# Compressed-block attention: the empty rows zeroed through the gate instead of a mask product, and all evictions of the second v half on ScalarE

## The chip, the core and the metric

The kernel runs on one core of a Trainium2 chip. The core has five engines with a queue each: TensorE (PE in the profile; PEld is its weight load), VectorE (DVE), ScalarE (ACT), GpSimd (POOL) and SyncE (SP), which issues DMAs. The metric is the device time of one execution in microseconds; of several executions the median counts.

## The reference, cut to what matters

Two layers of a decoder trunk on 512 tokens of width 1024 in float32: a convolution module with a SwiGLU feed-forward layer (FFN), then native sparse attention with another FFN. The change lies in the attention, in its branch over compressed blocks:

```
def masked_softmax(s, mask):
    s = jnp.where(mask, s.astype(jnp.float32), NEG_INF)
    return jax.nn.softmax(s, axis=-1) * mask.astype(jnp.float32)
...
    gates = jax.nn.sigmoid(proj[..., qd + kvd:].astype(jnp.float32)).reshape(bsz, seq, 3, H)
...
        s_c = jnp.einsum('bgrqd,bgnd->bgrqn', qc, k_cmp) * scale
        p_c = masked_softmax(s_c, cmp_end[None, :] <= t[:, None])
        o_c = jnp.einsum('bgrqn,bgnd->bgrqd', p_c, v_cmp)
...
        return g[0] * o_c + g[1] * o_s + g[2] * o_w
```

There are 31 compressed blocks of 32 tokens at a stride of 16. The first 31 tokens have no finished block: all their scores are masked, and p_c is zero there. With 512 tokens the selected and the window branch (o_s, o_w) each see every earlier token. There are 16 heads in 4 groups of keys and values.

## The kernel before, in words

Activations lie transposed in SBUF, as 8 tiles of 128 features by 512 tokens. Weights come by DMA in units of 128x1024, and each unit is split into a high part (ScalarE, tile wh) and a low part (VectorE, tile wl, function w_lo), so that three fast matmuls make one of nearly full precision.

The attention (function nsa) has these stages. First the projections to k and q, one tile of 128 features after the other. Then the projections to v and to the gates, in two halves: v_half(0) makes the first v and the gates, v_half(1) the second v. Each half runs over three weight units and four tiles of tokens (t = 0 to 3), and ends with v_evac, which brings the four results from PSUM to SBUF with a scale per token; EVAC_V says for each half which t VectorE takes, the others go to ScalarE. Third comes a loop over n = 1 to 17 that works 16 units: for each of 8 head pairs j (two heads of two groups) the selected and the window branch. In step n PE makes the scores of unit n (function score, tile S; par is the head of the pair, t the tile of query tokens, in the order 3, 2, 1, 0), transposes the probabilities of unit n-1 (function flip, PSUM tile T, SBUF tile t) and multiplies those of unit n-2 with v (function values, tile O). Behind each score, VectorE adds the mask and takes the extremum in one instruction (Pm<-S,mask, with mx), ScalarE takes the Exp with the row sum (Pm, sm), VectorE the reciprocal of sm, and GpSimd scales Pm by it and by the gate (function weigh, called some way behind through weigh_late). The score tiles rotate through three PSUM buffers in the loop: two of pool apS, and one of apS2, which is opened in the place of a bank that held the second v half.

The compressed branch is worked for two tiles j at a time, by q_pair(p), p = 0 to 3: scores makes 128 x 4 x 2 x 64 scores (tile sc; psc in PSUM), soft_a takes the maximum (cm) and the difference on VectorE and lets ScalarE take the Exp, soft_b multiplies with the mask of ones and zeros (C_CMUL, on GpSimd), soft_c takes the row sum (cl), the maximum of it with 0.5, the reciprocal and the product with the gate on VectorE, and scales sc by it on GpSimd; trans transposes the result (pct, pch, pcl) for its product with the compressed v. stacks makes the stacked q operands (tile St, part of it on GpSimd for p > 0).

The order of the work is written out by hand: every instruction between the second q tile and the end of the loop is kept in the order of the program on its engine. Pieces named by short words are hung into it. V_BESIDE gives for v_half(0) and v_half(1), for each weight unit and each t, what is issued ahead of that t's matmuls: for pair 0, "sa sb" (soft_a, soft_b) ahead of t = 1 in the second unit of v_half(0), with "r13" (a rotation of q, tiles qraw), "c1" (a chain of small VectorE instructions, rsy) and "w" (w_lo of the next unit) behind them; "gb" (the last part of the gates' sigmoid) and "sc cu" (soft_c, then what was put off) in v_half(1). FILL gives what run_fill issues, twice in each step of the loop: the first time ahead of the two flips that VectorE copies, the second time at the end of the scores, ahead of the flips that ScalarE copies. "P1.2" is the third part of pair 1: for pairs 1 to 3, part 2 is the move of q and soft_a, part 3 is stacks and soft_b, part 4 is soft_c, part 5 is trans. Parts 2 and 4 fall into the second slot of a step, part 3 into the first slot of the next one. What is wrapped in behind(...) is put off to the next run_fill, whose first act it is (catch_up): so soft_a's Exp is issued on ScalarE at the start of the slot in which part 3 runs, behind the first transposes' copy.

Of the kernel before, what the change touches and what calls it, by code (L numbers as in the profile page):

```python
# [10 lines left out]
F32 = mybir.dt.float32  # L11
# [4 lines left out]
ALU = mybir.AluOpType  # L16
AX = mybir.AxisListType
PSUM = bass.MemoryType.PSUM

P = 128  # L20
# [23 lines left out]
C_CMUL = C_CADD + 256  # L44
# [44 lines left out]
V_BESIDE = (  # L89
    (("w r12", "st0", "p2m", "sABCD a1"), ("w sa sb", "t1", "r13 c1", ""), ("w", "", "", "")),  # L90
    (("ga", "w", "s0", "s1 b1"), ("", "s2 s3 w", "gb s4 l", "s5 st1"), ("s6 l", "s7 l", "sc cu", "")))
EVAC_V = ((1, 3), (1, 3))
V_BANK = (2, 3, 0, 1)
STK_P = (0,)

# [53 lines left out]
def trunk(ctx: ExitStack, tc: tile.TileContext, A, out):  # L149
    order = [False]  # L150
    nc = Engines(tc, order)
# [9 lines left out]
    def nm(s):  # L161
        cnt[0] += 1
        return f"{s}_{cnt[0]}"
# [118 lines left out]
    cc = cst.tile([P, NCST], F32, name="cc")  # L282
# [820 lines left out]
    def nsa(acc, cosT, sinT, gnext):  # L1103
        cx = ExitStack()

        def pool(cxx, name, bufs, **kw):
            return cxx.enter_context(tc.tile_pool(name=name, bufs=bufs, **kw))
# [80 lines left out]
        qk = pool(qx, "qk", 1, side="right", reuse_waits="tile")  # L1188
# [21 lines left out]
        box = {}  # L1210
# [37 lines left out]
        def behind(f):  # L1248

            if box.get("steps"):  # L1250
                later.append(f)
            else:
                f()
# [132 lines left out]
        def pe(ins):  # L1386
            return ins if order[0] else tc.keep_in_program_order(ins)

        def q_pair(p):

            a = p // 2
            sc = qk.tile([P, 4, 2, 64], F32, tag="sc", name=nm("sc"), bufs=1)

            def move(jj):
                q = oT[2 * p + jj]
                box["q2", jj] = []
                for par in range(2):
                    hs = slice(par * 64, par * 64 + 64)
                    q2 = qk.tile([P, T], F32, tag="q2", name=nm("q2"), bufs=Q2B)
                    for half in range(2):  # L1400
                        nc.sync.dma_start(q2[half * 64:half * 64 + 64], q[hs])
                    box["q2", jj].append(q2)

            def stacks(jj):
                j = 2 * p + jj
                S2 = qk.tile([P, 1088], F32R, tag="S", name=nm("St"), bufs=3)
                for par in range(2):
                    ls = slice(64 - par * 64, 128 - par * 64)
                    q2 = box["q2", jj][par]
                    S = S2[:, par * T:par * T + T]  # L1410
                    if p > 0 and par in STK_P:
                        nc.gpsimd.tensor_copy(S, q2)
                        nc.gpsimd.tensor_tensor(S[ls], q2[ls], S[ls], ALU.subtract)
                    else:
                        nc.scalar.activation(S, q2, AF.Copy)
                        behind(lambda S=S, q2=q2, ls=ls: nc.vector.tensor_tensor(S[ls], q2[ls], S[ls], ALU.subtract))
                    qst[j, par] = S

            def scores(jj):
                q = oT[2 * p + jj]  # L1420
                ps = p2.tile([P, 4, 64], F32, tag="p2", name=nm("psc"))
                for t in range(4):
                    pe(nc.tensor.matmul(ps[:, t, :], q[:, t * P:(t + 1) * P], kcb[a], start=True, stop=True))
                nc.vector.scalar_tensor_tensor(
                    sc[:, :, jj, :], ps, -1.0,
                    cc[:, C_CADD:C_CADD + 256].rearrange("p (t n) -> p t n", t=4), ALU.mult, ALU.add)

            def soft_a():
                s3 = sc.rearrange("p t j (h n) -> p (t j h) n", h=2)
                m = qk.tile([P, 16 + APART], F32, tag="cm", name=nm("cm"), bufs=1)[:, :16]  # L1430
                nc.vector.tensor_reduce(m, s3, AX.X, ALU.max)
                nc.vector.tensor_tensor(s3, s3, m.unsqueeze(2).to_broadcast([P, 16, 32]), ALU.subtract)
                sf = sc.rearrange("p t j n -> p (t j n)")
                behind(lambda: nc.scalar.activation(sf, sf, AF.Exp))

            def soft_b():
                s5 = sc.rearrange("p t j (h n) -> p t (j h) n", h=2)
                nc.gpsimd.tensor_tensor(
                    s5, s5, cc[:, C_CMUL:C_CMUL + 128].rearrange("p (t n) -> p t n", t=4)
                    .unsqueeze(2).to_broadcast([P, 4, 4, 32]), ALU.mult)  # L1440

            def soft_c():
                s3 = sc.rearrange("p t j (h n) -> p (t j h) n", h=2)
                l = qk.tile([P, 16], F32, tag="cl", name=nm("cl"), bufs=1)
                nc.vector.tensor_reduce(l, s3, AX.X, ALU.add)
                nc.vector.tensor_scalar(l, l, 0.5, None, ALU.max)
                nc.vector.reciprocal(l, l)
                r0 = 2 * (p % 2)
                gv = gates[:, :, 8 * a:8 * a + 8].rearrange("p t (h r) -> p t r h", h=2)[:, :, r0:r0 + 2, :]
                lv = l.rearrange("p (t j h) -> p t j h", t=4, j=2)  # L1450
                nc.vector.tensor_tensor(lv, lv, gv, ALU.mult)
                nc.gpsimd.tensor_tensor(
                    s3, s3, l.unsqueeze(2).to_broadcast([P, 16, 32]), ALU.mult)

            def trans():
                pt = p2.tile([P, T], F32, tag="p2", name=nm("pct"))
                for t in range(4):
                    pe(nc.tensor.transpose(pt[:, t * P:(t + 1) * P], sc[:, t].rearrange("p j n -> p (j n)"), ident))
                ph = q3[1].tile([P, T], F32R, tag="pch", name=nm("pch"))
                pl = q3[1].tile([P, T], F32R, tag="pcl", name=nm("pcl"))  # L1460
                nc.scalar.activation(ph, pt, AF.Copy)
                behind(lambda: nc.vector.tensor_tensor(pl, pt, ph, ALU.subtract))
                pcT[p] = (ph, pl)

            if p == 0:
                return move, scores, stacks, soft_a, soft_b, soft_c, trans
            return [lambda: (move(0), scores(0)), lambda: (stacks(0), scores(1)), lambda: (move(1), soft_a()),
                    lambda: (stacks(1), soft_b()), soft_c, trans]

        extra, bcs = {}, {}  # L1470
# [72 lines left out]
        for e in range(2, 14):  # L1543
# [7 lines left out]
            n = state["next"]  # L1551
# [18 lines left out]
        gates = ap_.tile([P, 4, 48], F32, name="gates")  # L1570
# [15 lines left out]
        def v_evac(hf, pst):  # L1586
            br = 1 + hf
            z = vf[br] = ap_.tile([P, 4, 256], F32, tag="w1v", name=f"v{br}", bufs=2)
            for t in range(4):
                ps = pst[t]  # L1590
                r1 = rt[:, t:t + 1]
                if t in EVAC_V[hf]:
                    nc.vector.tensor_scalar(z[:, t], ps[:, :256], r1, None, ALU.mult)
# [19 lines left out]
        def sigm_b():  # L1613
            g2 = gates.rearrange("p a b -> p (a b)")
            nc.vector.tensor_scalar(g2, g2, 1.0, None, ALU.add)
            nc.vector.reciprocal(g2, g2)

        extra["ga"] = sigm_a
        extra["gb"] = sigm_b
# [222 lines left out]
    acc = ffn(acc, V_NM1, 0, lambda: rope.extend(rope_tables()))  # L1842
    cosT, sinT = rope
    acc = nsa(acc, cosT, sinT, V_NF1)
    ffn(acc, None, 1)
    hx[0].close()
# [162 lines left out]
```

## Time and profile before

| what | value |
|---|---|
| median of 3 runs | 1217.6 us (1212.36, 1217.6, 1219.96) |
| the profiled execution: time, span | 1220.19 us, 1218.4 us |
| granted TensorE clock, mean | 1.000 |
| PE busy, 650 to 690 us | 37.16 of 40 us |
| PE busy, 690 to 720 us | 28.21 of 30 us |
| PE busy, 760 to 800 us | 38.52 of 40 us |
| PE busy, 870 us to the end (output projection, second FFN) | 343.43 of 348.40 us |

The span runs from the first to the last instruction of the profiled execution. In a row of a timeline the columns are: start in us from the span's start, duration in us, engine, line, operation, output <- inputs by the names of the tiles, shape, count, and in brackets the idle time of the engine ahead of it with what ended it. Nearly all rows have line 136, that of the helper which records each instruction, so the tiles tell which is which. A row of the chain gives the start, the time that the piece adds to the chain, the engine and the tile. In a row of the waits stand the waiting instruction, what it waited for, the total in us, the number of times and the longest. The durations of matmuls are modelled, and one may start before the one ahead of it shows its end.

### The profile page before, as it was taken

The numbers are of one execution on the slowest core, as the hardware profiler recorded it, in microseconds if no ns is written. First come the engines' busy times: TensorE is split into PE (matmuls) and PEld (weight loads), VectorE is DVE, ScalarE is ACT, GpSimd is POOL, SyncE is SP. The second block draws the span as 40 slices with busy tenths as digits, with TensorE's granted clock in tenths as the row PEclk, the third lists the DMA queues.
The fourth block names the chain that finished last, engine by engine and source line by source line (L and its number), as shares of the span: only waits on it lengthen the run. The fifth ranks groups of instructions, "written<-read, shape, count | busy, mean of one in ns | idle before, by whom it ended". The sixth has DMA issues, their size and how long they took to land.

```text
span 1218.4 us, 20771 instructions
## 1 busy us (share of the span) xinstructions
PE 1193.8 (98%) x8015; PEld 1021.8 (84%) x8015; DVE 813.0 (67%) x1453; ACT 560.9 (46%) x1048; POOL 373.2 (31%) x403
## 2 busy tenths in 40 slices
PE   9999899999999999999999999999999999999998
PEld 6888678799999988888778767778879999998887
DVE  6879687878788665334677778764597766656221
ACT  6222454454455543233434687773354555544111
POOL 1039021144444301101232577752213444410000
PEclk9999999999999999999999999999999999999999
DMA  9636336346677323334354211112634877722331
GB/s 365 245 107 142 78 102 192 104 128 184 173 182 182 95 89 108 97 116 109 112 127 121 62 40 30 28 36 70 190 104 117 220 186 185 187 81 96 115 113 45
DMA packets 81539, 154.25 MB, mean 127 GB/s; under 512 B 36128, under 2 KB 37024, under 8 KB 80672
## 3 DMA queue, kind: packets, MB, share of 16 engines
q1 hardware_dynamic: 66096, 109.04, 28.7%
q0 software_dynamic: 15344, 43.88, 15.3%
q8 instruction: 63, 1.03, 0.4%
q14 instruction: 36, 0.29, 0.1%
HBM read 139.37 MB, written 5.28 MB: 119 GB/s over the span
## 4 chain that ended last, share of the span: by engine, by line
PE 76%; issue 8%; POOL 6%; DVE 6%; ACT 3%; DMA 1%; SPq 0%; POOLq 0%; DVEq 0%; ACTq 0%
PE st L136 35%; PE pp L136 28%; POOL S L136 6%; PE cpe L136 2%; PE O L136 2%; PE S L136 2%; PE pv L136 2%; PE T L136 2%; ACT Pm L136 1%; DVE Pm L136 1%; DVE c L136 1%; DVE t L136 1%; POOL Pm L136 1%; DVE St L136 0%; PE psc L136 0%
## 5 line engine op out<-in xcount | busy, mean ns | idle before, releaser
L136 ACT ACTIVATE wh<-wr 128x1024 fp32r<-128x1024 f32 (+3 forms) x158 | 160.4, 1015 | 294.5 <-PE st L136 140.2
L136 DVE TENSOR_TENSOR wl<-wr,wh 128x1024 fp32r<-128x1024 f32 (+3 forms) x158 | 185.4, 1173 | 128.7 <-ACT wh L136 128.5
L136 PE MATMUL st<-bh,sh 128*128 128x256 f32 x680 | 191.9, 282 | 2.9 <-DVE t L136 2.6
L136 PE MATMUL st<-bh,sl 128*128 128x256 f32 x680 | 190.0, 279 | 1.1 <-DVE sl L136 1.1
L136 PE MATMUL st<-bl,sh 128*128 128x256 f32 x680 | 189.7, 279 | 0.0
L136 PE MATMUL pp<-hh,wh 128*128 128x512 f32 x416 | 165.4, 398 | 2.1 <-ACT wh L136 1.5
L136 PE MATMUL pp<-hl,wh 128*128 128x512 f32 x416 | 163.2, 392 | 0.3 <-DVE hl L136 0.3
L136 PE MATMUL pp<-hh,wl 128*128 128x512 f32 x416 | 163.3, 393 | 0.1
L136 DVE TENSOR_TENSOR sl<-S,sh 128x512 fp32r<-128x512 f32 x136 | 115.5, 886 | 47.8 <-ACT sh L136 46.6
L136 POOL TENSOR_TENSOR S<-S,wr 128x512 f32<-128x512 f32 x68 | 106.4, 1564 | 132.0 <-DMA wr<-fw_in 69.3
L136 PE MATMUL st<-ah,wl 128*128 128x512 f32 x352 | 138.7, 394 | 0.0
L136 PE MATMUL st<-al,wh 128*128 128x512 f32 x352 | 138.0, 392 | 0.0
L136 PE MATMUL st<-ah,wh 128*128 128x512 f32 x352 | 136.6, 388 | 0.0
L136 PEld LDWEIGHTS st<-bh,sh 128*128 128x128 f32 x680 | 127.5, 187 | 6.0 <-DVE t L136 3.9
L136 PEld LDWEIGHTS st<-bh,sl 128*128 128x128 f32 x680 | 127.7, 188 | 1.5 <-DVE sl L136 1.5
L136 PEld LDWEIGHTS st<-bl,sh 128*128 128x128 f32 x680 | 127.5, 187 | 0.1
L136 POOL DMA_DIRECT2D S<-fw_x x68 | 60.6, 891 | 142.8 <-DMA S<-fw_x 141.7
L136 POOL TENSOR_SCALAR Pm<-Pm,sm,gates 128x512 f32<-128x512 f32 (+3 forms) x128 | 83.5, 664 | 49.0 <-DVE sm L136 31.7
L136 PEld LDWEIGHTS pp<-hh,wh 128*128 128x128 f32 x416 | 78.1, 188 | 23.9 <-issue 3.7
L136 PEld LDWEIGHTS pp<-hl,wh 128*128 128x128 f32 x416 | 78.2, 188 | 17.5 <-DVE hl L136 0.6
L136 PEld LDWEIGHTS pp<-hh,wl 128*128 128x128 f32 x416 | 78.2, 188 | 16.9 <-DVE wl L136 0.4
L136 POOL TENSOR_TENSOR acc<-acc,sq 128x512 f32<-128x512 f32 x18 | 31.7, 1762 | 191.4 <-ACT sq L136 178.0
(256 smaller groups left out, 2453.7 us busy)
## 6 DMA issues: line engine op xcount, KB each, us to landing
S<-fw_x POOLq DMA_DIRECT2D x68, 512.0 KB, 6.0
wr<-fw_in SPq DMA_DIRECT2D x46, 512.0 KB
wr<-fw_o SPq DMA_DIRECT2D x32, 512.0 KB
r<-fw_x SPq DMA_DIRECT2D x34, 256.0 KB
bd<-bands POOLq DMA_DIRECT2D x6, 1280.0 KB, 17.6
wr<-cw_in SPq DMA_DIRECT2D x14, 512.0 KB
wr<-fw_o SPq DMA_DIRECT2D x16, 384.0 KB
wr<-fw_s SPq DMA_DIRECT2D x8, 512.0 KB
```

Source lines behind the costliest of these rows:

```text
L136: z = f(*a, **kw)
```

## The change

Three things are changed. The row sum and the reciprocal move from soft_c to soft_b, where they take the place of GpSimd's product with the mask; the maximum with 0.5 goes. A row with no finished block then keeps its Exp values, and so that its result is still zero, the gates of the compressed branch (the first 16 columns of each token tile) are multiplied once, after the sigmoid, with the mask's first column, which is zero for tokens that have no finished block. And in the second v half all four evictions go to ScalarE.

```
@@ -89,7 +89,7 @@
-EVAC_V = ((1, 3), (1, 3))
+EVAC_V = ((1, 3), ())
@@ -1434,17 +1434,14 @@
             def soft_b():
-                s5 = sc.rearrange("p t j (h n) -> p t (j h) n", h=2)
-                nc.gpsimd.tensor_tensor(
-                    s5, s5, cc[:, C_CMUL:C_CMUL + 128].rearrange("p (t n) -> p t n", t=4)
-                    .unsqueeze(2).to_broadcast([P, 4, 4, 32]), ALU.mult)
+                s3 = sc.rearrange("p t j (h n) -> p (t j h) n", h=2)
+                l = box["cl"] = qk.tile([P, 16], F32, tag="cl", name=nm("cl"), bufs=1)
+                nc.vector.tensor_reduce(l, s3, AX.X, ALU.add)
+                nc.vector.reciprocal(l, l)
 
             def soft_c():
                 s3 = sc.rearrange("p t j (h n) -> p (t j h) n", h=2)
-                l = qk.tile([P, 16], F32, tag="cl", name=nm("cl"), bufs=1)
-                nc.vector.tensor_reduce(l, s3, AX.X, ALU.add)
-                nc.vector.tensor_scalar(l, l, 0.5, None, ALU.max)
-                nc.vector.reciprocal(l, l)
+                l = box["cl"]
                 r0 = 2 * (p % 2)
@@ -1614,6 +1611,8 @@
             nc.vector.reciprocal(g2, g2)
+            some = cc[:, C_CMUL:C_CMUL + 128].rearrange("p (t n) -> p t n", t=4)[:, :, :1]
+            nc.vector.tensor_tensor(gates[:, :, :16], gates[:, :, :16], some.to_broadcast([P, 4, 16]), ALU.mult)
```

## The prediction

> **What bounds the kernel now.** I read the page first (busy shares, chain), then the chain of waits between 640 and 860 us, and then the timelines of single engines around the three kinds of places that the diff touches.
>
> ```profile
> PE 1193.8 (98%) x8015; PEld 1021.8 (84%) x8015; DVE 813.0 (67%) x1453; ACT 560.9 (46%) x1048; POOL 373.2 (31%) x403
> PE 76%; issue 8%; POOL 6%; DVE 6%; ACT 3%; DMA 1%; SPq 0%; POOLq 0%; DVEq 0%; ACTq 0%
> ```
>
> TensorE (PE) carries the whole, but the average hides the attention stage. The compressed scores of head pairs 1, 2 and 3 are worked in between the big softmaxes near 703, 739 and 776 us, and there the chain leaves PE. For pair 3:
>
> ```profile
> 778.71 0.48 ACT t L136
> 779.19 0.52 ACT sc L136
> ...
> 782.32 0.61 DVE cl L136
> 784.12 1.84 POOL Pm L136 x3
> 785.97 1.01 POOL sc L136
> ```
>
> "ACT sc" is the Exp of the compressed scores, "DVE cl" the row sum, "POOL sc" the scaling by gate over sum. So ScalarE, VectorE and GpSimd hand the work around, and PE waits for GpSimd's scaled probabilities (Pm). The waits from 690 to 800 us, in a row (total, times, longest), and the two waits of pair 3, on PE:
>
> ```profile
> PE T L136 <- POOL Pm L136: 2.3, 6, 0.6
> ...
> 785.10 0.39 PE L136 MATMUL T<-cc,Pm 128*128 128x128 f32 x2
> 786.02 0.88 PE L136 MATMUL T<-cc,Pm 128*128 128x128 f32 x6 [0.53 <-POOL Pm L136]
> ...
> 787.57 0.66 PE L136 MATMUL T<-cc,Pm 128*128 128x128 f32 x4 [0.20 <-POOL Pm L136]
> ```
>
> Two waits a pair, 2.3 us for all three: that is all the slack that PE has in front of GpSimd there.
>
> **The change, part 1: sums moved forward, product with the mask gone (pairs 1 to 3).** Removed, four times: one GpSimd product and one VectorE max with 0.5. Moved: the row sum and its reciprocal, on VectorE, from soft_c into soft_b, which is a fill slot earlier. In that slot the queue of each engine stands in the order of the program. VectorE's, around pair 3, before:
>
> ```profile
> 777.97 0.69 DVE L136 COPY t<-T 128x512 f32<-128x512 f32 x1 [0.49 <-PE T L136]
> ...
> 778.64 0.67 DVE L136 CUSTOM_DVE_ANT_0 Pm<-S,mask 128x512 f32<-128x512 f32 x1
> ...
> 781.57 0.17 DVE L136 RECIPROCAL sm<-sm 128x2 f32<-128x2 f32 x1 [0.56 <-ACT Pm L136]
> ...
> 782.24 0.67 DVE L136 TENSOR_REDUCE cl<-sc 128x16 f32<-128x512 f32 x1
> 782.95 0.19 DVE L136 TENSOR_SCALAR cl<-cl 128x16 f32<-128x16 f32 x1
> ...
> 783.46 0.18 DVE L136 TENSOR_TENSOR cl<-cl,gates 128x16 f32<-128x16 f32 x1
> ```
>
> soft_b runs in the first fill slot of the step, and that stands in front of the COPY at 777.97. So the new sum is queued ahead of it, and the sum needs the Exp, which ScalarE reaches only later:
>
> ```profile
> 779.10 0.62 ACT L136 ACTIVATE sc<-sc 128x512 f32<-128x512 f32 x1
> ...
> 780.13 0.71 ACT L136 ACTIVATE Pm<-Pm,mx 128x512 f32<-128x512 f32 x1
> ```
>
> The Exp ends at 779.72; the sum starts 0.07 later (as GpSimd does behind the Exp of pair 0, below), at 779.79; 0.71 to the next instruction as in the rows, and 0.17 for the reciprocal as at 781.57: the COPY starts at 780.67 instead of 777.97, **2.70 us late**. Behind it wait the score reduction that stood at 778.64 (now 781.34), and with it ScalarE's 780.13, and PE's last score of the step, which needs the score buffer that this reduction frees (three rotate):
>
> ```profile
> 779.38 0.39 PE L136 MATMUL S<-kst,St 128*128 128x256 f32 x1
> ...
> 780.37 1.30 POOL L136 TENSOR_TENSOR sc<-sc,cc 128x512 f32<-128x512 f32 x1
> 781.66 4.31 POOL L136 TENSOR_SCALAR Pm<-Pm,sm,gates 128x512 f32<-128x512 f32 x6
> ```
>
> That score goes from 779.38 to 782.08, also 2.70. From there to 785.10 PE shows no other wait, so it brings all of this to the transposes. What comes back: GpSimd, without its 1.30 us product, starts the six Pm when the reciprocal of sm comes, at 781.4 at the earliest and so at most 0.25 sooner than 781.66, but it need not be sooner: it is done near 785.7, and PE now comes at 788.0. So both of PE's waits vanish, and nothing else does. The 1.2 us that VectorE no longer spends in soft_c (782.24 to 783.46) and its own wait of 0.56 let VectorE catch up before PE, but PE is last. Three pairs: 3 x 2.70 - 2.3 = **+5.8 us**. Bounds: none of the delay (VectorE finds the Exp done) gives -2.3; all of it with no wait given back gives +8.1. I take 5.8, since each row says in which order they stand.
>
> The Trainium skill (PSUM — Partial Sum Buffer, Engine vs sequencer instructions) says that the queues of ScalarE, VectorE and GpSimd are strict FIFO. This rule speaks against the change, and the 0.56 at 781.57, with the sum behind it idle too, agrees; if it did not hold here, the sum of this part would be the -2.3.
>
> **Part 2: pair 0.** Here soft_b follows soft_a at once:
>
> ```profile
> 660.59 0.68 DVE L136 TENSOR_TENSOR qraw<-qraw,cosT 128x512 f32<-128x512 f32 x1
> ...
> 662.20 1.05 DVE L136 TENSOR_SCALAR rsy<-qb 128x32 int32<-128x32 int32 x1
> 663.29 0.25 DVE L136 TENSOR_SCALAR rsy<-rsy 128x32 int32<-128x32 int32 x1
> ...
> 665.78 0.95 DVE L136 TENSOR_TENSOR wl<-wr,wh 128x768 fp32r<-128x768 f32 x1
> ...
> 660.70 0.64 ACT L136 ACTIVATE sc<-sc 128x512 f32<-128x512 f32 x1 [0.88 <-DVE sc L136]
> ...
> 661.41 1.80 POOL L136 TENSOR_TENSOR sc<-sc,cc 128x512 f32<-128x512 f32 x1 [3.38 <-ACT sc L136]
> ...
> 667.02 0.28 PE L136 MATMUL pv<-wl,hh 128*128 128x256 f32 x1
> ```
>
> VectorE would take 661.41 (GpSimd's start) for the sum, and the rotation that stood at 660.59 starts at 661.41 + 0.71 + 0.17 = 662.29, 1.7 late. VectorE is then without a gap up to wl, which PE needs at 667.02; wl ended at 666.73, 0.3 before. But the 1.05 us at 662.20 stands beside GpSimd's product, where its twin takes 0.25; with the product gone I take 0.8 back. wl ends 0.9 later, PE waits 0.9 - 0.3, with the semaphore **+0.7 us** (bounds 0 and, if the 1.05 stays, 1.5).
>
> The skill (SBUF — State Buffer, Who interferes with whom) has VectorE and GpSimd share a port pair under an exclusive lock. By it the 0.8 comes back; by the row alone, as a chance neighbour, it would not, and this part would be +1.5.
>
> **Part 3: end of the second v half.** VectorE loses two evictions, and the sum, max and reciprocal of pair 0 are no longer here:
>
> ```profile
> 679.34 0.67 DVE L136 TENSOR_REDUCE cl<-sc 128x16 f32<-128x512 f32 x1
> ...
> 680.88 0.32 DVE L136 TENSOR_TENSOR cl<-cl,gates 128x16 f32<-128x16 f32 x1
> 681.23 2.14 DVE L136 TENSOR_TENSOR St<-q,St 64x512 fp32r<-64x512 f32 x2
> 683.29 0.86 DVE L136 TENSOR_SCALAR v<-pv,rsy 128x256 f32<-128x256 f32 x2
> 684.08 0.67 DVE L136 CUSTOM_DVE_ANT_0 Pm<-S,mask 128x512 f32<-128x512 f32 x1
> ...
> 681.11 0.48 ACT L136 ACTIVATE v<-pv,rsy 128x256 f32<-128x256 f32 x1 [0.22 <-PE pv L136]
> 684.79 0.72 ACT L136 ACTIVATE Pm<-Pm,mx 128x512 f32<-128x512 f32 x1 [3.21 <-DVE mx L136]
> ...
> 681.14 0.39 PE L136 MATMUL S<-kl,St 128*128 128x512 f32 x1
> ...
> 683.82 0.39 PE L136 MATMUL S<-kst,St 128*128 128x256 f32 x1 [1.94 <-DVE v L136]
> ...
> 684.81 0.38 PE L136 MATMUL S<-kst,St 128*128 128x256 f32 x1 [0.50 <-DVE mx L136]
> ```
>
> This is VectorE's own stretch on the chain, and here the change pays: 1.54 (679.34 to 680.88) and 0.79 (683.29 to 684.08) fall out, the reduction at 684.08 moves to 681.75, and PE's score at 684.81 with it. The two evictions cost ScalarE 0.48 each, inside its idle 3.21 us; without that cover they would cost 0.96. ScalarE is through with all four by 682.1, and the next Pm comes at 682.4. If the two St get faster too, the score that the reduction reads, which PE ends at 681.53, stops the gain at 2.5. **-2.4 us** (bounds -1.4, if ScalarE's two stood in the way, and -2.5).
>
> The new product on the gates is not in the trace: 128x64 with two inputs; the cl product above (128x16) took 0.18 to 0.32, the wl one (128x768) 0.95. I take 0.25, nearest the small one. It follows the gates' reciprocal near 676.5, and soon behind it VectorE waits for PE anyway:
>
> ```profile
> 678.12 0.42 DVE L136 CUSTOM_DVE_ANT_0 Pm<-S,mask 128x256 f32<-128x256 f32 x1 [0.48 <-PE S L136]
> ```
>
> Those 0.48 hide it, so 0; without them it is 0.25, and at most 0.95 - 0.48 shows. The change issues no DMA and takes none past another; SP's queue stays as it is.
>
> **Sum:** 5.8 + 0.7 - 2.4 = +4.1 us. The profiled execution took 1220.19 us (span 1218.4 and 1.8 around it), 2.6 above the median of the runs shown, so 1224.3 for it and **1221.7** against the median of 1217.6.
>
> **The rivals.**
> (a) *Faster, by GpSimd.* If the delay at the COPY is smaller than the waits that it replaces (0.77 a pair), the shorter GpSimd chain decides: -2.3 and -2.4 with pair 0 hidden, -4.7, 1212.9. For it: GpSimd's Pm are what PE waits for. Against it: the Exp's end at 779.72 lies 1.75 behind the COPY's start. The whole turns at a COPY delay of (2.4 - 0.7 + 2.3) / 3 = 1.3 us; I read 2.70.
> (b) *The gain of part 3 does not come.* PE's scores then wait for ScalarE's evictions in place of VectorE's, as banks must come free: +6.5, 1224.1. For it: PE's 1.94 names the eviction. Against: ScalarE is idle for 3.21.
> (c) *Nothing given back:* +8.1 + 1.5 - 2.4 = 7.2, 1224.8. The waits for GpSimd would have to come back, since the reciprocals of sm are late as well. Against: PE is 2 us later than GpSimd's end.
> (d) *It does nothing,* as delay and gain stand even, 1217.6: for that each pair would have to lose 0.57, which no row gives.
>
> **Chances.** Forecast 0.55, (a) 0.15, (b) 0.08, (c) 0.10, (d) 0.12. The three runs of before lie 7.6 apart, 0.6%, so 1% (12 us) is about what can be told from no change. All cases lie within it: faster by over 1% 0.02, within 0.95, slower 0.03. The range goes from (a) at 1213 to (c) with some scatter of the runs, 1228; the forecast's own is 1219 to 1225.
>
> **What would show it.** In the profile after: a cl reduction on VectorE right behind the Exp, with some 2 us idle in front of it, released by "ACT sc", three times; a COPY of t behind it; PE waiting for "DVE mx" with S by 2 to 3 us per pair, and no more T waits for "POOL Pm"; near 667 a PE wait for wl of 0.7; near 682 no wait of PE for "DVE v". I am wrong if the sum finds the Exp done (no idle in front of it), or if PE does not stop behind the late reduction.

## The result and the profile after

The changed kernel takes 1223.75 us (median of 8 runs, 1220.06 to 1230.23), the kernel before in the same session 1217.84 (8 runs, 1212.36 to 1225.0). The ratio is 1.0051 with a 95% interval of 1.0027 to 1.0074: half a per cent slower, about 6 us (3.3 to 9.0 by the interval). The forecast was 1221.7, 4.1 more than the median then known, in a range of 1213 to 1228. The interval holds both the forecast's +4.1 and the +7.2 of rival (c), so the times alone do not choose between them; the traces do. The profiled execution took 1224.58 us, with a span of 1222.8.

The busy shares on the profile's page, after:

```profile
PE 1196.7 (98%) x8015; PEld 1025.1 (84%) x8015; DVE 816.7 (67%) x1448; ACT 561.7 (46%) x1050; POOL 369.7 (30%) x399
```

GpSimd has lost its four products (403 to 399 instructions). That tells nothing of the 6 us; the waits do. The largest of PE's waits between 655 and 820 us, first before, then after (total, times, longest):

```profile
PE T L136 <- POOL Pm L136: 2.3, 6, 0.6
PE S L136 <- DVE v L136: 1.9, 1, 1.9
PE T L136 <- DVE qraw L136: 1.7, 2, 1.0
PE S L136 <- DVE mx L136: 0.5, 1, 0.5
...
```

```profile
PE S L136 <- DVE mx L136: 8.1, 4, 2.6
PE T L136 <- DVE qraw L136: 1.9, 2, 1.1
...
PE pv L136 <- DVE wl L136: 0.4, 1, 0.4
...
```

The six waits for GpSimd's Pm are gone, and so is the one for the eviction (DVE v). In their place stand 8.1 us of waits for "DVE mx", the extremum that comes out of the score reduction: 0.4 of it behind the second v half, the rest in three halts, one for each of pairs 1 to 3. Pair 3 on VectorE, then the halt on PE and the transposes behind it:

```profile
777.79 0.69 DVE L136 TENSOR_REDUCE cl<-sc 128x16 f32<-128x512 f32 x1 [2.27 <-ACT sc L136]
778.51 0.25 DVE L136 RECIPROCAL cl<-cl 128x16 f32<-128x16 f32 x1
778.68 0.63 DVE L136 COPY t<-T 128x512 f32<-128x512 f32 x1
...
779.29 0.67 DVE L136 CUSTOM_DVE_ANT_0 Pm<-S,mask 128x512 f32<-128x512 f32 x1
```

```profile
780.02 0.39 PE L136 MATMUL S<-kst,St 128*128 128x256 f32 x1 [2.56 <-DVE mx L136]
...
785.74 1.04 PE L136 MATMUL T<-cc,Pm 128*128 128x128 f32 x8
...
787.08 0.60 PE L136 MATMUL T<-cc,Pm 128*128 128x128 f32 x4
```

VectorE stands idle for 2.27 us with the sum at the head of its queue; the COPY, the score reduction and through it PE's score come behind. The transposes at 785.74 and 787.08 wait for nothing.

For the rest, times are compared within one **stretch**: from the first 256-wide matmul of the second v half to the first matmul of the output projection. All that the diff touches lies in it but pair 0's soft_a and soft_b, just ahead of it. Its row in the table by windows, before and after (length, busy time of PE, PEld, VectorE, ScalarE and GpSimd with counts, granted clock, DMA share, GB/s), and three short windows of after:

```profile
666.90:821.81 154.91, 147.23 (x1026) 112.51 (x1024) 117.22 (x419) 117.41 (x342) 102.93 (x147) 1.00 0.16 42
```

```profile
661.33:821.60 160.27, 148.56 (x1027) 114.01 (x1025) 114.67 (x413) 118.54 (x344) 99.17 (x144) 0.99 0.15 41
738.00:741.00 3.00, 1.53 (x12) 1.44 (x13) 3.00 (x12) 1.23 (x3) 1.97 (x4) 0.98 0.01 3
741.00:744.00 3.00, 3.00 (x11) 2.16 (x11) 2.46 (x12) 3.00 (x10) 2.75 (x4) 0.50 0.00 0
744.00:747.00 3.00, 3.00 (x21) 1.60 (x22) 0.07 (x1) 1.42 (x6) 1.37 (x3) 0.95 0.00 0
```

The stretch grew by 5.36 us, close to the 5.9 by which the medians differ. But one row was not foreseen: behind pair 2's halt the granted clock stands at 0.50 for 3 us, and PE issues 11 matmuls where the next window has 21. Over the three windows (0.02 + 0.50 + 0.05) x 3 = 1.7 us of clock are missing.

### The profile page after: what moved, and what is told of

The parts are those of the page before. It is cut to its first block, busy times and chain, and to the rows that moved or that the text cites. A ratio compares the mean times of both kernels' runs of the same rounds, so it can differ in the third digit from the quotient of the medians.

```text
span 1222.8 us, 20769 instructions
## 1 busy us (share of the span) xinstructions
PE 1196.7 (98%) x8015; PEld 1025.1 (84%) x8015; DVE 816.7 (67%) x1448; ACT 561.7 (46%) x1050; POOL 369.7 (30%) x399
## 4 chain that ended last, share of the span: by engine, by line
PE 77%; issue 8%; DVE 6%; POOL 5%; ACT 3%; DMA 1%; SPq 0%; POOLq 0%; DVEq 0%; ACTq 0%
PE st L136 35%; PE pp L136 29%; POOL S L136 5%; PE O L136 3%; PE S L136 2%; PE cpe L136 2%; PE T L136 2%; ACT Pm L136 1%; DVE Pm L136 1%; DVE c L136 1%; DVE t L136 1%; PE pv L136 1%; DVE wl L136 1%; DVE St L136 1%; PE psc L136 0%
## 5 line engine op out<-in xcount | busy, mean ns | idle before, releaser
L136 DVE TENSOR_TENSOR sl<-S,sh 128x512 fp32r<-128x512 f32 x136 | 129.8, 986 | 54.5 <-ACT sh L136 52.2
L136 POOL TENSOR_TENSOR S<-S,wr 128x512 f32<-128x512 f32 x68 | 112.0, 1648 | 118.4 <-DMA wr<-fw_in 68.0
L136 ACT ACTIVATE sh<-S 128x512 fp32r<-128x512 f32 x136 | 80.0, 621 | 28.3 <-POOL S L136 28.3
```

What stands on the lines that cost most here:

```text
L136: z = f(*a, **kw)
```

## The experiments

The theory: the moved sum costs by standing at the head of VectorE's queue before its input is there, and it is the waiting, not the work, that PE pays for. Its rival (G in the expectations): the moved work itself costs, or the change's other parts do (evictions, gates, GpSimd). Each kernel computes the whole reference. Every profile is set against the stretch of 154.91 before and of 160.27 after; the ratios are to the kernel before on the same chip.

**The sum back in soft_c** (gates and evictions as in the changed kernel).

```
 def soft_b():
-    l = box["cl"] = ...; tensor_reduce(l, s3); reciprocal(l)
+    pass
 def soft_c():
-    l = box["cl"]
+    l = ...; tensor_reduce(l, s3); reciprocal(l)
```

> The changed kernel, with row sum and reciprocal back in soft_c; the product with the mask stays away and the gates stay zeroed. Measured by the stretch from the first matmul of the second v half to the first of the output projection: 155.0 us before, 160.3 after. Theory W (VectorE stands at the sum, waiting for the Exp): nothing waits, PE's waits for GpSimd go (-2.3), the two evictions and the max are gone from VectorE (-1.3): 151.4, and no idle of VectorE released by the Exp. Rival G (the moved work itself, wherever it stands, and the gate product cost the time): above 157. Total: -3.6 against before by W.

Measured: ratio 0.9978 (0.9956 to 0.9999), 1215.73 us; the stretch is 152.06, 0.7 above the 151.4 expected. The stretch and PE's longest waits:

```profile
663.71:815.77 152.06, 146.48 (x1026) 113.02 (x1024) 116.70 (x413) 117.11 (x342) 98.76 (x144) 1.00 0.16 42
```

```profile
PE S L136 <- DVE mx L136: 2.0, 1, 2.0
PE T L136 <- DVE qraw L136: 1.9, 2, 1.1
```

No wait for GpSimd and no halt at the pairs: 8.2 us of the stretch (160.27 - 152.06, the 1.7 of the clock among them) hang on where the sum stands, and what is left of the change is a gain of 2.85. With pair 0's sum still at the end of the v half, PE waits there 2.0 in one piece, where it had 1.9 and 0.5, and its score behind that (680.96, so 17.25 from the start of the stretch; 17.91 before) comes 0.66 sooner. The other 2.2 come later, where the waits for GpSimd (2.3) were.

**The wait alone.** The kernel before, with a small copy of the Exp's result in the place where the changed kernel has the sum; nothing reads the copy.

```
 def soft_b():
+    if p > 0:
+        look = qk.tile([P, 16], F32, tag="look", ...)
+        nc.vector.tensor_copy(look, sc.rearrange("p t j (h n) -> p (t j h) n", h=2)[:, :, 0])
     s5 = sc.rearrange("p t j (h n) -> p t (j h) n", h=2)
```

> The kernel before, with one small VectorE copy (128x16 of the scores behind the Exp, into a tile that nothing reads) in the slot of soft_b for pairs 1 to 3; everything else as before, the product with the mask too. Theory W: the copy waits for the Exp as the sum does, the COPY behind it is 2.0 us late, PE stands 2.0 and gets back its waits for GpSimd: +1.3 a pair, stretch 159, total +4. Rival G: three copies of 0.2: stretch 155.6, total +0.6 at most.

Measured: ratio 1.0037 (1.0014 to 1.0059), 1221.07 us, slower without a single moved sum. VectorE at pair 3 with GpSimd's instruction beside it, and the windows of the stretch and of three places at halts:

```profile
784.37 0.57 DVE L136 COPY look<-sc 128x16 f32<-128x16 f32 x1 [2.26 <-ACT sc L136]
784.86 0.68 DVE L136 COPY t<-T 128x512 f32<-128x512 f32 x1
...
783.63 1.27 POOL L136 TENSOR_TENSOR St<-q,St 64x512 fp32r<-64x512 f32 x1
```

```profile
665.81:829.40 163.59, 151.50 (x1026) 117.13 (x1024) 119.61 (x422) 117.94 (x342) 102.79 (x147) 0.97 0.16 40
684.00:688.00 4.00, 3.98 (x21) 3.29 (x20) 1.92 (x10) 2.98 (x10) 1.28 (x3) 0.57 0.15 35
704.00:708.00 4.00, 2.02 (x15) 1.67 (x13) 1.74 (x6) 2.88 (x9) 3.71 (x5) 1.00 0.01 2
708.00:712.00 4.00, 3.72 (x16) 3.53 (x17) 3.73 (x14) 3.42 (x11) 4.00 (x7) 0.57 0.00 0
```

The copy waits as the sum did (2.26 against 2.27), and PE halts three times for up to 2.3. So the wait does it, not the sum's 0.9 us. (The copy also holds back GpSimd's product with the mask, which writes what the copy reads; but PE has no wait for Pm in this trace.) The stretch is 4.6 longer than the 159 expected. The clock fell three times in it: at 684, behind the halt at the end of the v half, and at 708 (0.43 x 4 = 1.7 each), and near 788 (0.83 and 0.75 over 4 us each, 1.7). That is 5.1 us of clock, enough for the whole miss. The copy took 0.57 where I had put 0.2; in all three places it ends within 0.04 us of the end of a GpSimd product that ran beside it (for pair 3 at 784.94 and 784.90).

**Sums where VectorE has time.** Pairs 1 to 3 in soft_c; pair 0's soft_b moved from the first v half to the second, ahead of "b1".

```
-    ... ("w sa sb", "t1", "r13 c1", "") ...
-    (("ga", "w", "s0", "s1 b1"), ...
+    ... ("w sa", "t1", "r13 c1", "") ...
+    (("ga", "w", "s0", "s1 sb b1"), ...
 def soft_b():
+    if p == 0: row_sum()
 def soft_c():
+    if p > 0: row_sum()
```

> The changed kernel with the sums where VectorE has time: pair 0 ahead of the broadcast in the second v half (VectorE idles 1.26 us there), pairs 1 to 3 back in soft_c. Theory W: all gains and no wait: -2.4 and -2.3, stretch 150.3, total -4.7 against before. Rival G: above 157.

Measured: ratio 0.9961 (0.9935 to 0.9987), 1212.79 us; the stretch, and pair 0's sum in its new place:

```profile
665.50:815.83 150.33, 146.74 (x1027) 113.06 (x1025) 115.64 (x413) 117.22 (x343) 99.25 (x144) 1.00 0.16 43
```

```profile
670.09 0.68 DVE L136 TENSOR_REDUCE cl<-sc 128x16 f32<-128x512 f32 x1
...
671.43 0.68 DVE L136 SCALAR_TENSOR_TENSOR qys<-qyt,qys 32x512 fp32r<-32x512 f32 x1 [0.37 <-ACT qys L136]
```

The sum starts without a wait, and VectorE is idle again shortly behind it. 150.33 against 150.3 expected: the gain of part 3 and the end of GpSimd's waits add up (4.6), once nothing waits at the head of the queue.

**The same, but pair 0's soft_b left in the first v half** ("w sa sb" and "s1 b1" as in the changed kernel, row_sum() as above).

> The changed kernel with the sums of pairs 1 to 3 back in soft_c, that of pair 0 left where the change put it. Against run e5 (pair 0 in a gap: 150.3) it shows pair 0's wait alone: PE waits 0.5 to 0.7 for wl at the start of the second v half: stretch 150.9. The difference to the changed kernel (160.3) is then the part of pairs 1 to 3 with the clock. If pair 0 is what costs (rival), it stays above 155.

Measured: ratio 0.994 (0.9917 to 0.9964), 1210.83 us.

```profile
661.32:812.28 150.96, 146.96 (x1026) 113.03 (x1025) 116.02 (x413) 117.78 (x344) 99.20 (x144) 1.00 0.16 43
```

```profile
PE T L136 <- DVE qraw L136: 1.9, 2, 1.1
...
PE pv L136 <- DVE wl L136: 0.4, 1, 0.4
```

This differs from the changed kernel in pairs 1 to 3 alone, by 9.3 us of stretch. Less the 1.7 of the clock fall these are 7.6, close to the three halts that were measured (2.60, 2.56 and 2.56) and a little below the forecast's 3 x 2.70 = 8.1. Pair 0 by itself costs 0.63 (150.96 - 150.33), of which PE shows 0.4 as a wait for wl. By their ratios this kernel and the one above are both faster than before; their intervals overlap, so which is the better is open.

**The Exp at once.** The sum stays early, but ScalarE's Exp is issued in soft_a instead of at the next fill.

```
-    behind(lambda: nc.scalar.activation(sf, sf, AF.Exp))
+    nc.scalar.activation(sf, sf, AF.Exp)
```

> The changed kernel with one edit: the Exp of the compressed scores isn't put off to the next slot, so it is issued right behind the difference, into an idle 0.9 us of ScalarE, and is done before the sum is reached. Theory W: the sum costs only its own 0.9 us less VectorE's idle 0.5 there, less PE's waits for GpSimd: -0.3 a pair, -1.7 for the rest: stretch 152.4, total -2.6 against before. Rival G (it is the sum's work in front of the COPY): the stretch stays near 160. The throttled clock near the second pair goes as well by W, as PE no longer stands still.

Measured: ratio 1.0006 (0.998 to 1.0032), 1219.03 us; the stretch is 157.21, and 152.4 was expected: a miss of 4.8. On ScalarE at pair 3, and on PE:

```profile
771.98 0.63 ACT L136 ACTIVATE sc<-sc 128x512 f32<-128x512 f32 x1 [1.27 <-DVE sc L136]
772.52 1.07 ACT L136 ACTIVATE t<-T 128x512 f32<-128x512 f32 x2
```

```profile
773.15 1.56 PE L136 MATMUL O<-t,v 128*64 128x512 f32 x4 [1.24 <-ACT t L136]
```

The halt moved to another queue. Now the Exp stands at the head of ScalarE's queue and waits 1.27 us for soft_a's difference; the copies of t are behind it, and PE waits for them, 1.3 at most, three times, 3.8 us in all. The other 1.0 of the miss is not accounted for.

**The Exp behind ScalarE's copies.** The changed kernel again, but for pairs 1 to 3 the Exp is issued behind the flip that ScalarE copies in the same step.

```
-    behind(lambda: nc.scalar.activation(sf, sf, AF.Exp))
+    if p == 0: nc.scalar.activation(sf, sf, AF.Exp)
+    else: box["exp"] = lambda: nc.scalar.activation(sf, sf, AF.Exp)
...
     flip(((ub, 0),), "t0", nc.scalar)
+    if "exp" in box: box.pop("exp")()
```

> The changed kernel with the Exp of pairs 1 to 3 issued behind ScalarE's last two transposes' copies of the step, where ScalarE then idles 0.98 us, neither at once (run e3: it stood in front of those copies) nor put off. Theory W (a queue that stands at the waiting instruction costs the time): neither queue stands; the sum still comes ahead of the COPY: stretch 152.4, no wait of PE for t, granted clock 1.0. Rival G (the early sum's work, 0.9 us ahead of the COPY, is what costs): as e3, 157, or more.

Measured: ratio 0.9961 (0.994 to 0.9981), 1214.94 us; the stretch 151.72 (152.4 expected), and pair 3 on VectorE and PE:

```profile
767.93 0.68 DVE L136 TENSOR_REDUCE cl<-sc 128x16 f32<-128x512 f32 x1
...
768.81 0.63 DVE L136 COPY t<-T 128x512 f32<-128x512 f32 x1
```

```profile
770.15 0.39 PE L136 MATMUL S<-kst,St 128*128 128x256 f32 x1 [0.20 <-DVE mx L136]
```

Same sum, same early slot, and no idle time ahead of it, because its input is early too. PE waits 0.2 where the changed kernel has 2.56. That separates the place of the sum from its lateness: when the Exp is done, the early slot costs little. Against the kernel with late sums for these pairs (150.96) it is 0.76 us for the three.

**The evictions alone.** The kernel before with EVAC_V changed.

```
-EVAC_V = ((1, 3), (1, 3))
+EVAC_V = ((1, 3), ())
```

> The kernel before with only the second v half's evictions all on ScalarE. By the sum: VectorE loses 0.8 on its own stretch, ScalarE has idle time: stretch 154.1. Rival (PE waits for ScalarE's evictions instead): 155 or more.

Measured: ratio 0.9989 (0.9966 to 1.0011), not told from no change. The halt at the end of the v half, and the windows of the stretch and behind the halt:

```profile
676.74 0.39 PE L136 MATMUL S<-kst,St 128*128 128x256 f32 x1 [1.92 <-DVE mx L136]
```

```profile
659.60:814.92 155.32, 148.60 (x1026) 113.87 (x1024) 116.62 (x417) 117.96 (x344) 102.85 (x147) 0.99 0.16 42
677.54:680.95 3.41, 3.39 (x16) 2.70 (x14) 1.65 (x7) 2.43 (x8) 1.55 (x3) 0.50 0.24 55
```

With pair 0's sum still there PE halts for 1.92 in one piece, where it had 1.94 and 0.50. The score itself comes at 17.14 from the start of the stretch (676.74 - 659.60), where it came at 17.91: the evictions give 0.77, as expected. The clock fall behind the halt (0.50 x 3.41 = 1.7) takes it away in this profile: at the score of pair 1 PE is already 0.41 late, and it stays so to the end. So the 155.32 for an expected 154.1, which is the number that the rival named, comes from the clock and not from a wait for ScalarE's evictions.

**The changed kernel once more**, to see whether the clock falls again.

> The changed kernel once more, to see how often the granted clock falls behind PE's three halts: stretch 160.3 with one fall as in the first profile, 158.8 with none, 162 with two. If the clock's fall has nothing to do with the halts, it stands somewhere else this time.

Measured in one run: 1224.54 us.

```profile
663.13:824.96 161.83, 150.10 (x1027) 115.51 (x1025) 114.80 (x413) 118.66 (x344) 99.23 (x144) 0.98 0.15 40
700.00:704.00 4.00, 1.39 (x8) 1.19 (x8) 2.90 (x9) 2.27 (x6) 2.67 (x4) 0.90 0.00 2
704.00:708.00 4.00, 4.00 (x20) 3.40 (x20) 2.97 (x14) 3.60 (x11) 3.74 (x6) 0.67 0.00 0
744.00:748.00 4.00, 4.00 (x18) 2.91 (x17) 2.83 (x14) 4.00 (x12) 3.74 (x6) 0.57 0.00 0
```

This time it fell twice, at the halts of pairs 1 and 2, (0.10 + 0.33) x 4 and 0.43 x 4, 1.7 us each. The stretch is 1.56 longer than in the first profile, so one fall more costs PE about 1.6 of time.

## Why the prediction was right, and what its sum lacked

The same instructions of PE can be found in both traces. The table gives each by its distance from the start of the stretch (666.90 before, 661.33 after), and the forecast's running sum. Rows of both traces that stand nowhere yet, the scores of pairs 1 and 2, before and after:

```profile
705.89 0.38 PE L136 MATMUL S<-kst,St 128*128 128x256 f32 x1
...
742.14 0.39 PE L136 MATMUL S<-kst,St 128*128 128x256 f32 x1
```

```profile
661.98 0.39 PE L136 MATMUL pv<-wl,hh 128*128 128x256 f32 x1 [0.36 <-DVE wl L136]
...
677.55 0.39 PE L136 MATMUL S<-kst,St 128*128 128x256 f32 x1 [0.38 <-DVE mx L136]
...
701.49 0.38 PE L136 MATMUL S<-kst,St 128*128 128x256 f32 x1 [2.60 <-DVE mx L136]
...
739.47 0.39 PE L136 MATMUL S<-kst,St 128*128 128x256 f32 x1 [2.56 <-DVE mx L136]
```

| PE's instruction | before | after | later by | forecast |
|---|---|---|---|---|
| second matmul of the v half (wl) | 0.12 | 0.65 | +0.53 | +0.7 |
| score behind part 3 (684.81; 677.55) | 17.91 | 16.22 | -1.69 | 0.7 - 2.4 = -1.7 |
| score of pair 1 | 38.99 | 40.16 | +1.17 | +1.0 |
| score of pair 2 | 75.24 | 78.14 | +2.90 | +2.9 |
| score of pair 3 (779.38; 780.02) | 112.48 | 118.69 | +6.21 | +4.9 |
| last transposes of pair 3 (787.57; 787.08) | 120.67 | 125.75 | +5.08 | +4.1 |
| output projection | 154.91 | 160.27 | +5.36 | +4.1 |

Each forecast is the one above it with 2.70 more for a pair's halt and 0.77 less for its waits for GpSimd.

- **Part 1** was right in mechanism and nearly in size. Expected were halts of 2 to 3 us and 2.3 given back: the halts are 2.60, 2.56 and 2.56, and no wait for Pm is left. That the wait causes them is shown by the copy alone (it brings them) and by the Exp behind the copies (it takes them away with the sum in the same slot).
- **Part 2**: +0.53 for +0.7. The sum started as worked out, behind the Exp, and the 0.8 us that were to come back did. VectorE's sum, and its chain instruction that stood beside GpSimd's product (1.05 before), after:

```profile
655.81 0.69 DVE L136 TENSOR_REDUCE cl<-sc 128x16 f32<-128x512 f32 x1 [0.70 <-ACT sc L136]
...
658.32 0.18 DVE L136 TENSOR_SCALAR rsy<-qb 128x32 int32<-128x32 int32 x1
```

  It takes 0.18 with no GpSimd instruction beside it, and so it does in the five other kernels without the product; with the wait alone and with the evictions alone, which keep the product, it takes 1.05 again. The Trainium skill (SBUF — State Buffer, Who interferes with whom) says that the two engines share a port pair, that the one which issues first holds it for its whole instruction while the other is blocked, and that tensor_scalar is among the operations which can need it. The 1.05 agrees: it ended at 663.25, GpSimd's product at 663.21.
- **Part 3**: 0.53 down to -1.69 is -2.2, for -2.4. PE no longer waits for "DVE v". The evictions alone bring this score 0.77 sooner, where the prediction had 0.79; the rest, 1.45, is what pair 0's sum, max and reciprocal leave free, where it had 1.54. With all gains and no wait for wl (the sums where VectorE has time) the score comes at 15.59 from the start of the stretch (681.09), 2.32 sooner than before.
- **The gates' product** was put at 0.25 and hidden. It took 0.23, and VectorE still stands idle for PE behind it, 0.42 us at 674.12:

```profile
671.64 0.23 DVE L136 TENSOR_TENSOR gates<-gates,cc 128x64 f32<-128x64 f32 x1
```

- **What the sum lacked** is in one step of the table: from pair 2's score to pair 3's the lateness grows by 3.31, where 2.70 - 0.77 = 1.93 was forecast. In that step lie the 1.7 us of missing clock. Less these it is 1.6, a little below the forecast, as the step before is (1.73). The prediction took the clock as 1.00 throughout, as the row of before has it, and gave no term to a fall. One fall costs about 1.6 of time, by the two profiles of the changed kernel (161.83 - 160.27); without it the stretch would have grown by 3.8, for 4.1.
- **The rivals.** (a) needed a delay at the COPY below 1.3 us; with halts of 2.6 its gain never came, but the kernels that take the wait away give it (-4.6 in the stretch with sums in gaps, against the rival's -4.7). (b) falls with part 3's -2.2, and (d) with an interval of the ratio that leaves out 1. (c) comes near in time (1224.8), but not by its mechanism: it has the waits for GpSimd come back, and they did not. That the median came out nearer to (c)'s number than to the forecast's does not speak for (c): a clock fall, which no rival has, is worth about 1.6.
- **The wrong expectation** among the experiments is that of the Exp at once. It followed VectorE's queue and did not ask, as the prediction's own step did, what stands behind the moved instruction on ScalarE. The misses of the wait alone and of the evictions alone are clock falls.

## What to carry to other kernels

Before an instruction is moved forward in an engine's queue, ask when its input is ready, not whether the engine has time: 0.9 us of work cost three halts of 2.6, and a copy that nobody reads cost three of 2.2 to 2.3. The same question has to be put to the engine that makes the input. The gains of a change (here GpSimd's 2.3 and the 2.2 at the end of the v half) show in the time only when the moved work stands where its input is done: the same edits gave a ratio of 1.0051 (1.0027 to 1.0074) with early sums and 0.994 (0.9917 to 0.9964) with late ones for pairs 1 to 3. Of that difference, some 13 us, 9.3 lie in the stretch.

## What was not expected of the hardware

**The clock falls at halts of PE.** In all, seven falls were seen in the stretch: one in the changed kernel's first profile, two in its second, three with the wait alone, one with the evictions alone. Each lasts 3.41 us at 0.50, so that 1.7 us of clock are missing, and each begins between 0.2 us ahead of the end of a halt of 1.9 us or more and 1.5 us behind it. Not every such halt has one: of 13 halts between 1.9 and 2.6 us in these profiles and those of before and of the sum back in soft_c, 7 have a fall, and the 1.94 of before and the 2.0 of the sum back in soft_c have none. With halts of 1.3 at most (the kernel with sums where VectorE has time, the one like it, and the two with the Exp moved) there is none, and their stretches have a granted clock of 1.00.

Which halts have a fall can be read from the traces. The falls of one trace begin at whole multiples of 3.413 us from each other: at 684.21, 708.10 and 786.61 with the wait alone (7 and 23 steps), at 703.19 and 744.15 in the second profile of the changed kernel (12 steps). So a trace can be cut into windows of 3.413 us that end where a fall begins. The fullest window with a fall behind it (evictions alone) and the emptiest at a halt without one (wait alone, pair 2):

```profile
674.12:677.54 3.42, 1.50 (x12) 1.30 (x11) 3.39 (x10) 1.37 (x5) 1.41 (x1) 1.00 0.42 98
```

```profile
745.65:749.06 3.41, 1.64 (x12) 1.59 (x13) 3.41 (x13) 1.71 (x4) 3.23 (x5) 1.00 0.01 2
```

PE's busy time, the first figure behind the length, was 0.90 to 1.50 us in the seven windows ahead of a fall, and 1.64 or more in all windows of the other six halts (1.83 or more at the changed kernel's pairs 1 and 3, first profile). For before and the sum back in soft_c, whose only fall is at the program's end, windows laid from that fall give 1.94 and 2.28. So the halt's length alone does not decide. In these 13 it is how much of PE's idle time falls into one window: the changed kernel's halts of 2.6 us have a fall where 2.0 us or more of them lie in one window, and none where the larger part is 1.7 at most. The bound between 1.50 and 1.64 was found in these traces and tried on no others, and PE's busy time is modelled.

The Trainium skill (TensorE: Matmul & The Clock Gate, What's actually happening) describes a gate that halves the clock behind an idle window of about 3.4 us, the window running free of the program. The 0.50, the 3.41 us of a fall and the steps of 3.413 agree; but no window here was idle throughout, and in the one with the evictions alone PE was busy for 1.50 of 3.42 us. Its advice (Why this matters for your kernels) is to keep idle gaps below about 3 us; here gaps of 1.90 to 2.61 were followed by a fall, so by these runs that is too generous. A halt of set length and place by itself was not made; that the halt brings the fall rests on the order of the two and on the 13 halts.

**Time outside the stretch varies.** What lies ahead of it and behind it took 1057 to 1063.5 us in the ten profiles: 1063.5 before, 1062.5 after, 1057.3 with the evictions alone, though the order of the instructions there is the same. This is as large as the change itself, and it is not explained; it is why the profiles were compared by the stretch.
